# A hybrid decoder layer on one core: the mLSTM products in other PSUM banks, zeros and copies on GpSimd, attention's AV matmuls one step later

## The chip, the core and the metric

The kernel runs on one core of a Trainium2 chip. The core has TensorE (PE, matmuls into PSUM), VectorE (DVE), ScalarE (ACT), GpSimd (POOL) and SyncE (SP, which here only starts DMA transfers). Each engine works through its own list of instructions in order; semaphores let an instruction wait for another engine. PSUM has eight banks of 128 x 512 float32. The metric is the device time of one execution in microseconds, and the kernel before is the reference for it.

## What is computed

One decoder layer on 512 positions of width 1024, in float32. The normalised input goes through one projection; one group of its columns feeds four mLSTM heads, the other a sparse attention of eight heads whose keys an indexer selects (the 128 best of each query's past). Both results are concatenated, projected and added; a gated MLP with a short causal convolution and a last norm follow.

```python
h = rms_norm(x, norm_mix)
m_q, m_k, m_v, m_o, m_i, m_f, a_q, a_k, a_v, i_q, i_k, i_w = split_cols(h @ w_in, IN_SIZES)
qk = silu(causal_dwconv(concat(m_q, m_k), mlstm_conv_w, mlstm_conv_b))
hm = mlstm_chunkwise(q, k, v, m_i + i_bias, m_f + f_bias)       # 4 heads, 64 wide keys, 128 wide values
#   sc  = (q k^T / 8) * exp(dmat - m_t);  num = inter + sc v;  h = num / max(|den|, exp(-m_t))
hm = sigmoid(m_o) * rms_norm(hm, mlstm_norm)
ha = dsa_attention(a_q, a_k, a_v, i_q, rms_norm(i_k), i_w / sqrt(8), rel_bias)
#   score = sum_h relu(q_idx k_idx / 8) w;  top-k keys;  softmax(q k / 8 + bias) v
x = x + concat(hm, ha) @ w_out
u = causal_dwconv(rms_norm(x, norm_ffn) @ w_up, ffn_conv_w, ffn_conv_b)
out = rms_norm(x + (silu(gate) * val) @ w_down, norm_final)
```

## The kernel before

Matmuls run on pairs of rounded numbers: each float32 operand is split into a rounded high part and the rest (`split`, L121: ScalarE copies, VectorE or GpSimd subtracts), and three products make one. Weights come in pieces of 1 MB, are split into `whi` and `wlo`, and are used once. The 512 positions are four blocks (t = 0 to 3).

The order of the work is written out by hand. `merge` (L29) lays the steps of a main list (projection matmuls) and of side lists side by side: each side list has a range (a, b) as shares of the main list, and its steps are spread over it by their cost. What comes out is the order in which instructions are issued; each engine keeps it. So an instruction that waits holds up everything behind it on its engine. `later` holds small pieces (weight splits, convolution taps) that are issued after a step each.

PSUM banks come from rotating tags (L61): "mm" has two banks for projections, "lg" three, "tp" two, "av" one. A tile of a tag waits for the last reader of the tile that had the bank before.

Three stages matter here.

The stage of L734 to L744 ends with the first step of the attention loop (`ready`) and the first six of the 33 top-3 instructions (`top_steps(3)`: sixteen pairs of `max` and `match_replace` on VectorE over block 3's scores, then `keep`, the mask of the selected keys).

The stage of L857 to L862 has as its main list the mLSTM convolution projections and half of the values (24 steps); beside it run the other 27 top-3 instructions, the gates, two `decay` steps, and the attention loop `att_[1:]`. The loop has 32 items, one for each block t and head h. Its step i issues: the query halves for coming items (`queries`: ScalarE, GpSimd; `second`: the rounding rests, on VectorE into `qlz`, two at a time); the logits of item i on TensorE into a bank of "lg"; the transposes of item i-3 into "tp" and their copy to SBUF (pT, on ScalarE, for odd heads of block 3 on VectorE); the reduce of item i-1 on VectorE (L695) and its exponential on ScalarE (L698); for block 3 the score of item i on GpSimd (L704, bias plus mask, which the reduce of that item reads); and the AV matmuls of item i-4, followed after the eighth head by the division (L718).

The stage of L912 to L917 has 24 projection steps of twelve 256-column matmuls (the other half of the values, then the output gate). Beside it run two `decay` steps, `parts`, `qks` and four `to_mix`. `parts` first makes, for each of four heads, `keys(h)` (ScalarE copies, VectorE subtracts, giving kh) and then `queries(h)` (two ScalarE copies into the halves of qh, a VectorE subtract into ql); `zeros(h)` (L811) clears the other half of ql, heads 0 and 1 ahead of `keys(0)`, heads 2 and 3 behind `keys(3)`. `qks` has 16 products `qk(h, sb)`: two matmuls into one bank, and one or two multiplies on VectorE which read the bank. `to_mix` transposes an attention block into "tp" and splits it from there. The products and `to_mix` share "tp":

```python
pq = bank("tp")     # L844, in qk
pt = bank("tp")     # L906, in to_mix
```

Of the kernel before, what the change touches and what calls it, by code (L numbers as in the profile page):

```python
# [13 lines left out]
AF = mybir.ActivationFunctionType  # L14
# [30 lines left out]
def hybrid_layer(ctx: ExitStack, tc: tile.TileContext, a, out):  # L45
# [591 lines left out]
    def att_steps(ts):  # L637
# [21 lines left out]
        def step(i):  # L659
            if i % 4 == 1 and i // 4 + 1 < n // 4:  # L660
                queries(i // 4 + 1)
            if i and i % 2 == 0 and i // 2 + 1 < n // 2:
                second(i // 2 + 1)
            if i < n:
                t, h = items[i]
                w = (t + 1) * 128
# [21 lines left out]
            if 0 <= i - 1 < n:  # L688
                t, h = items[i - 1]
                w = (t + 1) * 128  # L690
                if h == 0:
                    rsum[t] = small.tile([128, 8], F32, name="rs")
                l = ap.tile([128, 512], F32, name="l", tag="wB", bufs=3)
                nm = small.tile([128, 1], F32, name="nm", bufs=4)
                nc.vector.tensor_tensor_reduce(l[:, :w], lg.pop(i - 1)[:, :w],  # L695
                                               backwards(bias["T"][:, h, :w]) if t < 3 else score[t], -1.0, 3.0e38,
                                               OP.add, OP.min, nm)
                nc.scalar.activation(l[:, :w], l[:, :w], AF.Exp, bias=nm, scale=-1.0,  # L698
                                     accum_out=rsum[t][:, h:h + 1])
                ll[i - 1] = l  # L700
            if i < n and items[i][0] >= 3:

                t, h = items[i]
                nc.gpsimd.tensor_tensor(score[t], backwards(bias["T"][:, h, :(t + 1) * 128]), keep[t], OP.add)  # L704
            if 0 <= i - 4 < n:
                t, h = items[i - 4]
                if h == 0:
                    pout[t] = bank("av")
                pT, po = lp.pop(i - 4), pout[t]
                for j in range(t + 1):  # L710
                    nc.tensor.matmul(po[:, h * 64:(h + 1) * 64], pT[:, j * 128:(j + 1) * 128],  # L711
                                     av[:, j, h * 64:(h + 1) * 64], start=(j == 0), stop=(j == t))
# [14 lines left out]
        def ready():  # L727
# [1 line left out]
            queries(0)  # L729
            second(0)  # L730
            second(1)
        return [ready] + [costed(i) for i in range(n + 4)]

    main = []  # L734
    for c in range(4):
# [46 lines left out]
    def weight_steps():  # L782
# [28 lines left out]
        def zeros(h):  # L811

            b_ = own[h % 2][1]
            if h == 2:
                ql["two"] = ap.tile([128, 2, S], F32R, name="mql", tag="mk")
            ql[h] = ql["two"][:, h - 2, :] if h >= 2 else ap.tile([128, S], F32R, name="mql", tag=("ql", "score3")[h])
            nc.scalar.activation(ql[h][b_].rearrange("p (t c) -> p t c", t=NB),
                                 ident[b_, None, :].to_broadcast([64, NB, 128]), AF.Copy, scale=0.0)

        def keys(h):  # L820
            if h == 0:
# [10 lines left out]
        def queries(h):  # L832
            a_, b_ = own[h % 2]
            qh[h], src = part(4 + h), mq[a_, h // 2, :]
            nc.scalar.activation(qh[h][a_], src, AF.Copy)
            nc.scalar.activation(qh[h][b_], src, AF.Copy)
            nc.vector.tensor_tensor(ql[h][a_], src, qh[h][a_].bitcast(F32), OP.subtract)

        def qk(h, sb):
# [1 line left out]
            n = (NB - sb) * 128  # L841
            t0 = min(sb * 128, 256)
            o, ks = sb * 128 - t0, slice(sb * 128, (sb + 1) * 128)
            pq = bank("tp")  # L844
            nc.tensor.matmul(pq[:, :S - t0], kh[h][:, ks], qh[h][:, t0:], start=True, stop=False)
            nc.tensor.matmul(pq[:, :S - t0], kh[h][:, ks], ql[h][:, t0:], start=False, stop=True)
            s_ = sc[:, sb * 128:(sb + 1) * 128]
# [11 lines left out]
    for c in range(4):  # L859
        main += fm_steps(H, to_conv(c))  # L860
    main += tm_steps(H, to_mv(0))
    merged(main, (0.0, 0.5, top3[6:]), (0.403, 0.74, gates_b), (0.781, 0.957, decays[:2]), (0.7, 0.7, [silus]), (0.007, 1.0, att_[1:]))  # L862


    def head_steps(pair):
# [47 lines left out]
    main = tm_steps(H, to_mv(1))  # L913
    for c2 in range(2):
        main += tm_steps(H, to_mo(c2))
    merged(main, (0.0, 0.05, decays[2:]), (0.08, 0.5, parts), (0.42, 1.0, qks),
           (0.16, 0.6, [lambda t=t: to_mix(ha[t], mixa, t) for t in range(NB)]))  # L917

    def gate_out(t):
# [202 lines left out]
```

## Time and profile before

| | value |
|---|---|
| time, three runs | 680.48 us median, 679.57 lowest, 1314.57 highest |
| profiled execution, its own time | 681.01 us |
| its span, from first to last instruction | 679.3 us |
| TensorE busy, share of the span | 656.2 us, 97% |
| VectorE busy | 398.9 us, 59% |
| ScalarE busy | 299.8 us, 44% |
| GpSimd busy | 147.5 us, 22% |
| mean granted clock of TensorE | 0.993 |
| slices of the span (of 40) with a granted clock under 0.9 | one, the fourteenth (about 221 to 238 us) |

Times of rows count from the span's start. "Busy" is the time in which an engine has an instruction in work; matmuls overlap, so a busy TensorE isn't at its peak. The granted clock is 1.00 at 2.4 GHz and 0.50 at 1.2 GHz. A row of a timeline has start and duration in us, engine, line, operation, written tile <- read tiles, shape, and how many instructions it stands for; in brackets, the idle time ahead of it and what ended that.

### The profile page before, as it was taken

The numbers are of one execution on the slowest core, as the hardware profiler recorded it, in microseconds if no ns is written. First come the engines' busy times: TensorE is split into PE (matmuls) and PEld (weight loads), VectorE is DVE, ScalarE is ACT, GpSimd is POOL, SyncE is SP. The second block draws the span as 40 slices with busy tenths as digits, with TensorE's granted clock in tenths as the row PEclk, the third lists the DMA queues.
The fourth block names the chain that finished last, engine by engine and source line by source line (L and its number), as shares of the span: only waits on it lengthen the run. The fifth ranks groups of instructions, "written<-read, shape, count | busy, mean of one in ns | idle before, by whom it ended". The sixth has DMA issues, their size and how long they took to land.

```text
span 679.3 us, 8957 instructions
## 1 busy us (share of the span) xinstructions
PE 656.2 (97%) x3455; PEld 560.0 (82%) x3455; DVE 398.9 (59%) x741; ACT 299.8 (44%) x516; POOL 147.5 (22%) x156
## 2 busy tenths in 40 slices
PE   7999999989999799999999999999999999999996
PEld 4987889778899698889888888888888888888885
DVE  4688999996656656656465655555555552222233
ACT  5555355655847424435434444445344441111223
POOL 2132576333430005314011010110101020000023
PEclk9999999999999799999999999999999999999999
DMA  9321533010111111132133213331233143323102
GB/s 305 115 65 62 190 122 124 0 64 11 52 63 63 62 64 62 35 122 68 58 123 119 67 63 125 124 106 54 89 124 123 66 152 124 124 73 114 62 32 93
DMA packets 47194, 62.22 MB, mean 92 GB/s; under 512 B 3795, under 2 KB 40855, under 8 KB 47152
## 3 DMA queue, kind: packets, MB, share of 16 engines
q1 hardware_dynamic: 45488, 56.83, 25.0%
q0 software_dynamic: 944, 3.25, 1.5%
q10 hardware_dynamic: 720, 1.57, 0.6%
q8 instruction: 27, 0.44, 0.3%
q14 instruction: 15, 0.12, 0.1%
HBM read 59.53 MB, written 2.12 MB: 91 GB/s over the span
## 4 chain that ended last, share of the span: by engine, by line
PE 74%; DVE 16%; ACT 4%; issue 3%; POOL 1%; DMA 1%; POOLq 0%; DVEq 0%; ACTq 0%
PE bank_mm L192 9%; PE bank_mm L193 9%; PE bank_mm L194 9%; PE bank_av L192 4%; PE bank_av L193 4%; PE bank_av L194 4%; DVE score L513 3%; DVE m L510 3%; DVE score L495 2%; PE bank_lg L1052 2%; PE bank_lg L1050 2%; PE bank_lg L1051 2%; PE bank_mm L363 2%; PE bank_av L711 2%; PE bank_mm L945 1%
## 5 line engine op out<-in xcount | busy, mean ns | idle before, releaser
L123 DVE TENSOR_TENSOR wlo<-raw,whi 128x1024 fp32r<-128x1024 f32 x78 | 96.7, 1244 | 121.5 <-ACT whi L122 121.5
L122 ACT ACTIVATE whi<-raw 128x1024 fp32r<-128x1024 f32 x100 | 104.9, 1051 | 95.2 <-PE bank_mm L1051 73.4
L192 PE MATMUL bank_mm<-fh,whi 128*128 128x512 f32 (+1 forms) x248 | 93.2, 376 | 0.0
L194 PE MATMUL bank_mm<-fh,wlo 128*128 128x512 f32 (+1 forms) x248 | 93.1, 376 | 0.0
L193 PE MATMUL bank_mm<-fl,whi 128*128 128x512 f32 (+1 forms) x248 | 93.1, 375 | 0.0
L1015 POOL TENSOR_TENSOR yc<-yc 128x512 f32<-128x512 f32 x22 | 28.4, 1291 | 213.4 <-DVE yc L999 213.4
L123 POOL TENSOR_TENSOR wlo<-raw,whi 128x1024 fp32r<-128x1024 f32 x22 | 54.2, 2465 | 75.9 <-ACT whi L122 58.6
L194 PEld LDWEIGHTS bank_mm<-fh,wlo 128*128 128x128 f32 x248 | 46.7, 188 | 8.5
L192 PEld LDWEIGHTS bank_mm<-fh,whi 128*128 128x128 f32 x248 | 46.7, 188 | 8.5
L193 PEld LDWEIGHTS bank_mm<-fl,whi 128*128 128x128 f32 x248 | 46.7, 188 | 8.3
L192 PE MATMUL bank_av<-fh,whi 128*128 128x512 f32 (+1 forms) x128 | 48.2, 376 | 0.0
L194 PE MATMUL bank_av<-fh,wlo 128*128 128x512 f32 (+1 forms) x128 | 48.1, 376 | 0.0
L193 PE MATMUL bank_av<-fl,whi 128*128 128x512 f32 (+1 forms) x128 | 48.1, 376 | 0.0
L122 ACT ACTIVATE gh<-yc 128x512 fp32r<-128x512 f32 x22 | 13.9, 632 | 69.2 <-POOL yc L1015 69.2
L192 PE MATMUL bank_mm<-hh,whi 128*128 128x512 f32 (+1 forms) x112 | 43.7, 390 | 0.0
L123 DVE TENSOR_TENSOR gl<-yc,gh 128x512 fp32r<-128x512 f32 x22 | 15.2, 693 | 47.4 <-ACT gh L122 47.4
L194 PE MATMUL bank_mm<-hh,wlo 128*128 128x512 f32 (+1 forms) x112 | 42.0, 375 | 0.0
L193 PE MATMUL bank_mm<-hl,whi 128*128 128x512 f32 (+1 forms) x112 | 42.0, 375 | 0.0
L236 PE MATMUL bank_mm<-whi,hh 128*128 128x256 f32 x112 | 33.0, 295 | 0.0
L1008 ACT ACTIVATE yc<-yc 128x512 f32<-128x512 f32 x22 | 13.9, 632 | 42.3 <-DVE yc L999 42.3
L237 PE MATMUL bank_mm<-whi,hl 128*128 128x256 f32 x112 | 32.0, 286 | 0.0
L238 PE MATMUL bank_mm<-wlo,hh 128*128 128x256 f32 x112 | 32.0, 286 | 0.0
(325 smaller groups left out, 1542.0 us busy)
## 6 DMA issues: line engine op xcount, KB each, us to landing
raw<-in_w_up_dram SPq DMA_DIRECT2D x22, 1024.0 KB, 5.1
raw<-in_w_in_dram SPq DMA_DIRECT2D x13, 1024.0 KB, 4.9
raw<-in_w_down_dram SPq DMA_DIRECT2D x11, 1024.0 KB, 4.9
raw<-in_w_out_dram SPq DMA_DIRECT2D x4, 1024.0 KB
T<-skew POOLq DMA_DIRECT2D x1, 2048.0 KB, 8.6
x<-in_x_dram SPq DMA_DIRECT2D x3, 512.0 KB, 5.3
out_dram<-xn SPq DMA_DIRECT2D x4, 256.0 KB, 2.1
out_dram<-xn ACTq DMA_DIRECT2D x4, 256.0 KB, 2.5
```

The costliest lines, as they stand in the source:

```text
L122: nc.scalar.activation(hv, src, AF.Copy)
L123: (eng or nc.vector).tensor_tensor(lv, src, hv.bitcast(F32), OP.subtract)
L192: nc.tensor.matmul(ps_, lh, rh, start=first, stop=False)
L193: nc.tensor.matmul(ps_, lh, rl, start=False, stop=False)
L194: nc.tensor.matmul(ps_, ll, rh, start=False, stop=last)
L236: nc.tensor.matmul(st["ps"], ah, wh[:, i, :], start=(k == 0), stop=False)
L237: nc.tensor.matmul(st["ps"], al, wh[:, i, :], start=False, stop=False)
L238: nc.tensor.matmul(st["ps"], ah, wl[:, i, :], start=False, stop=(k == 7))
L510: nc.vector.max(m8[0], acc)
L513: nc.vector.match_replace(acc, m8[0], acc, TAKEN)
L1008: nc.scalar.activation(ys[c][:, 0, :], ys[c][:, 0, :], AF.Silu)
L1015: nc.gpsimd.tensor_tensor(y[:, 0, :], y[:, 0, :], y[:, 1, :], OP.mult)
```

## The change

Five edits. In the attention loop `second` is issued after the reduce of the step, and the AV matmuls work on item i-5 in place of i-4, so that the loop has one step more. `zeros(h)` runs on GpSimd, and for heads 2 and 3 so does the second of the two query copies. The products take their bank from "lg". And three ranges move: top-3 to 0.57 from 0.5, `parts` to (0.05, 0.45) from (0.08, 0.5), `qks` to begin at 0.48 from 0.42.

```diff
--- before.py
+++ after.py
@@ -659,8 +659,6 @@
         def step(i):
             if i % 4 == 1 and i // 4 + 1 < n // 4:
                 queries(i // 4 + 1)
-            if i and i % 2 == 0 and i // 2 + 1 < n // 2:
-                second(i // 2 + 1)
             if i < n:
                 t, h = items[i]
                 w = (t + 1) * 128
@@ -698,15 +696,17 @@
                 nc.scalar.activation(l[:, :w], l[:, :w], AF.Exp, bias=nm, scale=-1.0,
                                      accum_out=rsum[t][:, h:h + 1])
                 ll[i - 1] = l
+            if i and i % 2 == 0 and i // 2 + 1 < n // 2:
+                second(i // 2 + 1)
             if i < n and items[i][0] >= 3:
 
                 t, h = items[i]
                 nc.gpsimd.tensor_tensor(score[t], backwards(bias["T"][:, h, :(t + 1) * 128]), keep[t], OP.add)
-            if 0 <= i - 4 < n:
-                t, h = items[i - 4]
+            if 0 <= i - 5 < n:
+                t, h = items[i - 5]
                 if h == 0:
                     pout[t] = bank("av")
-                pT, po = lp.pop(i - 4), pout[t]
+                pT, po = lp.pop(i - 5), pout[t]
                 for j in range(t + 1):
                     nc.tensor.matmul(po[:, h * 64:(h + 1) * 64], pT[:, j * 128:(j + 1) * 128],
                                      av[:, j, h * 64:(h + 1) * 64], start=(j == 0), stop=(j == t))
@@ -729,7 +729,7 @@
             queries(0)
             second(0)
             second(1)
-        return [ready] + [costed(i) for i in range(n + 4)]
+        return [ready] + [costed(i) for i in range(n + 5)]
 
     main = []
     for c in range(4):
@@ -814,8 +814,8 @@
             if h == 2:
                 ql["two"] = ap.tile([128, 2, S], F32R, name="mql", tag="mk")
             ql[h] = ql["two"][:, h - 2, :] if h >= 2 else ap.tile([128, S], F32R, name="mql", tag=("ql", "score3")[h])
-            nc.scalar.activation(ql[h][b_].rearrange("p (t c) -> p t c", t=NB),
-                                 ident[b_, None, :].to_broadcast([64, NB, 128]), AF.Copy, scale=0.0)
+            nc.gpsimd.tensor_scalar(ql[h][b_].rearrange("p (t c) -> p t c", t=NB),
+                                    ident[b_, None, :].to_broadcast([64, NB, 128]), 0.0, None, op0=OP.mult)
 
         def keys(h):
             if h == 0:
@@ -833,7 +833,10 @@
             a_, b_ = own[h % 2]
             qh[h], src = part(4 + h), mq[a_, h // 2, :]
             nc.scalar.activation(qh[h][a_], src, AF.Copy)
-            nc.scalar.activation(qh[h][b_], src, AF.Copy)
+            if h < 2:
+                nc.scalar.activation(qh[h][b_], src, AF.Copy)
+            else:
+                nc.gpsimd.tensor_copy(qh[h][b_], src)
             nc.vector.tensor_tensor(ql[h][a_], src, qh[h][a_].bitcast(F32), OP.subtract)
 
         def qk(h, sb):
@@ -841,7 +844,7 @@
             n = (NB - sb) * 128
             t0 = min(sb * 128, 256)
             o, ks = sb * 128 - t0, slice(sb * 128, (sb + 1) * 128)
-            pq = bank("tp")
+            pq = bank("lg")
             nc.tensor.matmul(pq[:, :S - t0], kh[h][:, ks], qh[h][:, t0:], start=True, stop=False)
             nc.tensor.matmul(pq[:, :S - t0], kh[h][:, ks], ql[h][:, t0:], start=False, stop=True)
             s_ = sc[:, sb * 128:(sb + 1) * 128]
@@ -859,7 +862,7 @@
     for c in range(4):
         main += fm_steps(H, to_conv(c))
     main += tm_steps(H, to_mv(0))
-    merged(main, (0.0, 0.5, top3[6:]), (0.403, 0.74, gates_b), (0.781, 0.957, decays[:2]), (0.7, 0.7, [silus]), (0.007, 1.0, att_[1:]))
+    merged(main, (0.0, 0.57, top3[6:]), (0.403, 0.74, gates_b), (0.781, 0.957, decays[:2]), (0.7, 0.7, [silus]), (0.007, 1.0, att_[1:]))
 
 
     def head_steps(pair):
@@ -913,7 +916,7 @@
     main = tm_steps(H, to_mv(1))
     for c2 in range(2):
         main += tm_steps(H, to_mo(c2))
-    merged(main, (0.0, 0.05, decays[2:]), (0.08, 0.5, parts), (0.42, 1.0, qks),
+    merged(main, (0.0, 0.05, decays[2:]), (0.05, 0.45, parts), (0.48, 1.0, qks),
            (0.16, 0.6, [lambda t=t: to_mix(ha[t], mixa, t) for t in range(NB)]))
 
     def gate_out(t):
```

Line numbers of the new kernel are 2 lower from L664 to L700, the same from there to L835, and 3 higher from L837. The order of instructions follows at three places.

The first place is TensorE in the third stage, where the products begin (`part` and `mql` are the parts of keys and queries; `bank_mm` and `bank_av` are projection banks). Before:

```order
L236 MATMUL bank_av<-whi,hh 128x256
L237 MATMUL bank_av<-whi,hl 128x256
L238 MATMUL bank_av<-wlo,hh 128x256
L845 MATMUL bank_tp<-part 128x512
L846 MATMUL bank_tp<-mql,part 128x512
L845 MATMUL bank_tp<-part 128x384
L846 MATMUL bank_tp<-mql,part 128x384
L236 MATMUL bank_av<-whi,hh 128x256
L237 MATMUL bank_av<-whi,hl 128x256
```

After, the first product:

```order
L238 MATMUL bank_av<-wlo,hh 128x256
L848 MATMUL bank_lg<-part 128x512
L849 MATMUL bank_lg<-mql,part 128x512
L236 MATMUL bank_mm<-whi,hh 128x256
L237 MATMUL bank_mm<-whi,hl 128x256
L238 MATMUL bank_mm<-wlo,hh 128x256
```

And after the twelve projection matmuls that begin there, the second and the third:

```order
L238 MATMUL bank_mm<-wlo,hh 128x256
L848 MATMUL bank_lg<-part 128x384
L849 MATMUL bank_lg<-mql,part 128x384
L911 MATMUL bank_tp<-ident,qv 128x128 x4
L848 MATMUL bank_lg<-part 128x256
L849 MATMUL bank_lg<-mql,part 128x256
L236 MATMUL bank_mm<-whi,hh 128x256
```

The first two products stood together on banks of "tp"; now a projection step stands between them, both are on "lg", and the fourth `to_mix` (L911, the only user of "tp") comes between the second and the third.

On ScalarE the same stage, from the third key copy to the third `to_mix` copy, before:

```order
L826 ACTIVATE part<-mk 64x512
L817 ACTIVATE mql<-ident 64x512 x2
L761 ACTIVATE mv<-bank_mm 128x2x128
L835 ACTIVATE part<-mq 64x512
L836 ACTIVATE part<-mq 64x512
L122 ACTIVATE mixa<-bank_tp 128x4x128
L835 ACTIVATE part<-mq 64x512
L836 ACTIVATE part<-mq 64x512
L122 ACTIVATE whi<-raw 128x1024 x2
L835 ACTIVATE part<-mq 64x512
L836 ACTIVATE part<-mq 64x512
L122 ACTIVATE mixa<-bank_tp 128x4x128
```

After:

```order
L826 ACTIVATE part<-mk 64x512
L761 ACTIVATE mv<-bank_av 128x2x128
L835 ACTIVATE part<-mq 64x512
L837 ACTIVATE part<-mq 64x512
L761 ACTIVATE mv<-bank_mm 128x2x128
L122 ACTIVATE mixa<-bank_tp 128x4x128
L835 ACTIVATE part<-mq 64x512
L837 ACTIVATE part<-mq 64x512
L835 ACTIVATE part<-mq 64x512
L122 ACTIVATE whi<-raw 128x1024 x2
L835 ACTIVATE part<-mq 64x512
L122 ACTIVATE mixa<-bank_tp 128x4x128 x2
```

The zeros (L817) are gone from between the key copies and the query copies, two of the second query copies (L836, now L837) as well, and the head-3 query copy (the last L835) stands ahead of the third `mixa` copy.

The second place is TensorE in the attention loop, one step of block 1 (the numbers tell tiles apart). Before, where pT_1513 is the copy of bank_tp_1510, transposed in the step before:

```order
L670 MATMUL bank_lg_1524<-kS_657,qd_1399 128x256
L671 MATMUL bank_lg_1524<-kS_657,ql_658 128x256
L673 LDWEIGHTS identb_356
L673 MATMUL bank_lg_1524<-keep1_366,identb_356 128x256
L681 MATMUL bank_tp_1528<-ident_117,l_1486 128x128 x2
L711 MATMUL bank_av_1490<-qv_84,pT_1513 128x64 x2
```

After, where pT_1524 is the copy of bank_tp_1521, and the step between has bank_tp_1547:

```order
L668 MATMUL bank_lg_1561<-kS_657,qd_1489 128x384
L669 MATMUL bank_lg_1561<-kS_657,ql_658 128x384
L671 LDWEIGHTS identb_356
L671 MATMUL bank_lg_1561<-keep2_367,identb_356 128x384
L679 MATMUL bank_tp_1565<-ident_117,l_1526 128x128 x2
L711 MATMUL bank_av_1507<-qv_84,pT_1524 128x64 x2
```

The AV matmul now reads what was transposed two steps before.

The third place is VectorE where `keep` of block 3 (keep_368) is written; L695, now L693, with T is a reduce of blocks 0 to 2, with score_365 of block 3. Before:

```order
L513 MATCH_REPLACE score_365<-m_1682,score_365 128x512
L516 TENSOR_SCALAR keep_368<-score_365 128x512
L755 SCALAR_TENSOR_TENSOR mk<-bank_mm,cw,mk 128x509
L695 ISA l,nm<-bank_lg,T 128x384
L695 ISA nm 128x1
L755 SCALAR_TENSOR_TENSOR mk<-bank_mm,cw,mk 128x510
L755 SCALAR_TENSOR_TENSOR mk<-bank_mm,cw,mk 128x511
L657 TENSOR_TENSOR ql<-qv,qd 64x128 x2
L695 ISA l,nm<-bank_lg,T 128x384
```

After:

```order
L510 MAX m_1750<-score_365 128x8
L513 MATCH_REPLACE score_365<-m_1750,score_365 128x512
L693 ISA l,nm<-bank_lg,T 128x384
L693 ISA nm 128x1
L516 TENSOR_SCALAR keep_368<-score_365 128x512
L693 ISA l,nm<-bank_lg,T 128x384
L693 ISA nm 128x1
L657 TENSOR_TENSOR ql<-qv,qd 64x128 x2
L693 ISA l,nm<-bank_lg,score_365 128x512
```

Before, four reduces of block 2 stood between `keep` and the first reduce that reads the score (two of them further down than is shown); now there is one.

## Rows read from the trace of the kernel before

**Rows 1.** Busy time by stretch: engine us (instructions), granted clock, DMA share, GB/s.
```profile
core 0: us, PE busy (x) PEld busy (x) DVE busy (x) ACT busy (x) POOL busy (x), PEclk, DMA share, GB/s
...
118.70:160.00 41.30, 37.61 (x230) 30.96 (x229) 37.74 (x115) 25.12 (x75) 11.75 (x15) 1.00 0.08 26
...
222.86:227.70 4.84, 0.00 (x1) 0.00 (x1) 3.94 (x6) 4.74 (x7) 0.00 (x0) 0.88 0.09 6
227.70:233.41 5.71, 5.71 (x25) 5.71 (x26) 2.83 (x8) 0.07 (x1) 0.00 (x0) 0.50 0.46 179
...
254.07:660.00 405.93, 405.93 (x1924) 340.86 (x1923) 202.56 (x276) 156.02 (x230) 58.17 (x67) 1.00 0.27 91
```

**Rows 2.** TensorE's waits, 118 to 250: who for whom, us, times, longest.
```profile
PE bank_tp L845 <- DVE mixa L123: 4.8, 1, 4.8
PE bank_av L711 <- ACT pT L686: 2.7, 4, 0.7
PE bank_lg L670 <- DVE nm L695: 1.0, 2, 0.6
PE bank_tp L681 <- ACT l L698: 0.8, 1, 0.8
PE bank_av L711 <- DVE qv L718: 0.4, 1, 0.4
```

**Rows 3.** Timeline of TensorE around the long wait.
```profile
227.70 0.69 PE L845 MATMUL bank_tp<-part 128*128 128x384 f32 x1 [4.84 <-DVE mixa L123]
...
228.51 0.41 PE L236 MATMUL bank_av<-whi,hh 128*128 128x256 f32 x1
...
231.07 0.41 PE L845 MATMUL bank_tp<-part 128*128 128x256 f32 x1
...
234.44 0.28 PE L236 MATMUL bank_mm<-whi,hh 128*128 128x256 f32 x1
...
235.87 0.41 PE L845 MATMUL bank_tp<-part 128*128 128x512 f32 x1
```

**Rows 4.** Timeline of ScalarE, 217.9 to 227.6.
```profile
217.99 1.27 ACT L817 ACTIVATE mql<-ident 64x512 fp32r<-64x512 f32 x2 [0.85 <-DVE part L827]
...
220.08 0.63 ACT L836 ACTIVATE part<-mq 64x512 fp32r<-64x512 f32 x1
...
225.87 0.60 ACT L122 ACTIVATE mixa<-bank_tp 128x512 fp32r<-128x512 f32 x1
```

**Rows 5.** Timeline of VectorE, 223.7 to 228.
```profile
224.90 0.42 DVE L767 COPY past<-bank_mm 128x256 f32<-128x256 f32 x1
...
226.97 0.67 DVE L123 TENSOR_TENSOR mixa<-bank_tp,mixa 128x512 fp32r<-128x512 f32 x1
```

**Rows 6.** Timelines of GpSimd and VectorE, 105 to 111, and GpSimd at 210.
```profile
105.70 1.51 POOL L634 TENSOR_SCALAR ql<-ident 128x512 fp32r<-128x512 f32 x1
...
106.23 0.69 DVE L621 TENSOR_TENSOR kS<-k__1054,kS 64x512 fp32r<-64x512 f32 x1
...
108.84 2.41 POOL L123 TENSOR_TENSOR wlo<-raw,whi 128x1024 fp32r<-128x1024 f32 x1 [0.71 <-PE bank_av L238]
108.93 2.46 DVE L657 TENSOR_TENSOR ql<-qv,qd 64x128 fp32r<-64x128 f32 x1
...
210.24 0.64 POOL L800 TENSOR_SCALAR_AFFINE_SELECT qv<-qv 128x512 f32<-128x512 f32 x1 [1.45 <-ACT qv L799]
```

**Rows 7.** Timeline of TensorE, 135 to 137, one attention step.
```profile
135.28 0.37 PE L670 MATMUL bank_lg<-kS,qd 128*128 128x256 f32 x1
...
135.72 0.38 PE L681 MATMUL bank_tp<-ident,l 128*128 128x128 f32 x2
136.84 0.41 PE L711 MATMUL bank_av<-qv,pT 128*128 128x64 f32 x2 [0.74 <-ACT pT L686]
```

**Rows 8.** Timelines of VectorE and GpSimd, 159 to 173: keep, score, its reduce.
```profile
159.11 0.43 DVE L516 TENSOR_SCALAR keep<-score 128x512 bf16<-128x512 f32 x1
...
167.86 1.18 POOL L704 TENSOR_TENSOR score<-T,keep 128x512 f32<-128x512 f32 x1
...
172.98 0.69 DVE L695 CUSTOM_DVE_ANT_0 l<-bank_lg,score 128x512 f32<-128x512 f32 x1
```

## The prediction

> **What bounds the kernel now.** I read the page first, then busy time by stretch, then TensorE's waits, then the timeline of the place that stands out. The stretches [rows 1] show where something can be won: from 254.07 to 660 us TensorE is busy for all 405.93 us, so what is won before 254 us is kept to the end, and nothing that this diff touches runs later. Up to 118.7 us both kernels issue the same rows. Between the two there are 41.30 us with TensorE busy for 37.61, a second half of the attention loop that is nearly full, then 4.84 us in which it does nothing, then 5.71 us at clock 0.50, the lower of its two levels (1.2 GHz).
>
> TensorE's waits of this part are five groups [rows 2]. One wait alone is 4.84 us: a product of `qk` (L845) for the subtract of `to_mix` (L123) on VectorE. The others, 2.7 + 1.0 + 0.8 + 0.4 = 4.9 us, belong to the attention loop: AV matmuls for the pT copy on ScalarE (four times), logits for a bank that VectorE has not reduced, one transpose for the exponential, one AV for the division.
>
> **What the 4.84 us are.** `qk` and `to_mix` both take "tp", which has two banks. The second product needs the bank of the third `to_mix`; that comes free when VectorE ends the subtract that starts at 226.97 and takes 0.67 [rows 5], and TensorE goes on at 227.70 [rows 3]. VectorE is late because ScalarE is: it copies that bank only at 225.87, after zeros, query copies, an earlier split and two weight splits in one unbroken queue from 217.99 [rows 4]. After the stall the clock is low: twelve 256-column matmuls take 231.07 - 228.51 = 2.56 us, the same twelve later 235.87 - 234.44 = 1.43 us [rows 3]. The low stretch lasts 5.71 us [rows 1], so it costs 5.71 x (1 - 1.43 / 2.56) = 2.5 us. The place costs 4.84 + 2.5 = 7.3 us in all.
>
> **Products in "lg", later.** "lg" has three banks, and in this stage only the four `decay` steps use it before. So the first three products find free banks whatever `to_mix` does, and the fourth needs the first one's. In the new order one more projection step (twelve matmuls, 1.43 us) stands ahead of the first product, which so ends at 222.86 + 1.43 = 224.3 in the old run's time. The fourth comes two steps of 1.43 us, two products and a group of transposes (some 0.8 us) later, near 227.9. Is the first bank read by then? In the old run VectorE read it straight after the subtract of 226.97. ScalarE's half of that split moves up: four zeros leave the queue ahead of it (two pairs of 1.27 us, whose starts overlap: 2.4 us) with the idle 0.85 us before the second pair, and one query copy of 0.63 us leaves while another moves in [rows 4]. So 225.87 becomes about 222.6. VectorE has one subtract (0.69 us for that shape, [rows 6]) and one bank copy (0.42, [rows 5]) more ahead of the read, and its weight splits in between; I put the read at 225 to 226.5, at least 1.4 us ahead of the fourth product. No wait takes the place of the stall, and without it I see no cause for the low clock, so I take the whole 7.3 us. The next thing to be late would be VectorE's copy of a projection bank: it came at 224.90 [rows 5], is needed again near 228, and moves up with the rest.
>
> **Zeros and copies on GpSimd.** A zeroing from the same source took 1.51 us there (L634, [rows 6]), against 0.63 on ScalarE [rows 4]. Four are 6.0 us. The two query copies I bound by ScalarE's 0.63 us from below and by 1.5 us from above, and take the upper end. GpSimd ends its last `affine_select` at 210.24 + 0.64 = 210.9 [rows 6]; zeros 0 and 1 then run to about 214, zeros 2 and 3 wait for the last key subtract and run to about 220, the copies to 223 at worst. The first product's second matmul needs the first block at about 224, head 2 comes many products later. That is ten microseconds of cover, and GpSimd has nothing else to do here. Cost: nothing; without the cover 1.5 us for each block.
>
> The trace has a warning for work that runs beside VectorE. While GpSimd did a two-input subtract (2.41 us from 108.84), a VectorE subtract with both inputs in SBUF took 2.46 us for a quarter of the elements of one that took 0.69. But that one of 0.69 us ran wholly inside GpSimd's zeroing of L634 [rows 6], which is work of the kind that is moved: one input. I go by this row. The Trainium skill ("SBUF — State Buffer", Who interferes with whom) makes no such difference: a VectorE instruction with two SBUF inputs contends with any GpSimd instruction that reads SBUF, and whoever issues second waits. By that rule the subtracts of this stage would be held up by the zeros, which is the third rival; the 2.46 us agree with it, the 0.69 us do not.
>
> **AV a step further back, `second` after the reduce.** The four pT waits are 0.7 us each. They stand where two attention steps follow one another without projection work: logits at 135.28, AV wanted at 136.10, begun at 136.84 [rows 7]. One step more is such a stretch of 0.8 us more, so all 2.7 us should go; if ScalarE is late by more than a step, none. `second` now runs behind the reduce of its step, so a reduce no longer waits for it, nor for a GpSimd instruction that blocks it. Of the logits' 1.0 us I keep half, because `max` and `match_replace` still stand among the reduces. At the exponential's wait (0.8) ScalarE ran a weight split and a bank copy first; in the new order the exponential comes ahead of them, and it goes. The division's 0.4 stays. Against this stands VectorE's load, 37.74 us in 41.30 [rows 1]: TensorE can't run much ahead of it. The range 0.57 for 0.5 spreads the same 27 top-3 instructions over 14% more work, which gives VectorE about what TensorE gains, and I take off 1.0 us. Sum 2.7 + 0.5 + 0.8 - 1.0 = 3.0 us, with bounds 0 and 4.9.
>
> The spread makes `keep` of block 3 late. It was written at 159.11; the score build (1.18 us on GpSimd) and the first reduce that needs it (172.98) came so much later that 12 us lay free between them [rows 8]. In the new order three more reduces, three convolution taps and a `second` stand ahead of `keep`, some 5 us of work, and one reduce lies between it and the one that needs it; the loop itself arrives some 4 us sooner, from the waits gone and from projection steps that now stand behind it. About 3 us of cover are left. I cost it at nothing, a miss at 1 to 2 us.
>
> **Sum.** The profiled execution took 681.0 us (span 679.3). 681.0 - 7.3 - 3.0 = 670.7. The median of the runs shown is 680.5, 0.5 lower: **670.2 us**.
>
> **Rivals.** First, the attention loop gives nothing: VectorE sets its pace and the waits form again. For it speaks VectorE at 91%; against it, that only 1.0 of the 4.9 us are waits on a reduce. 680.5 - 7.3 = 673.2.
>
> Second, the loop gives all 4.9: 680.5 - 7.3 - 4.9 = 668.3. For it, that nothing delays a reduce by a blocked subtract any more; against it, the division, which nothing touches.
>
> Third, the zeros block VectorE's subtracts. VectorE then loses 3.0 us to the first pair and up to 6.0 to the second with the copies. The cover of the fourth product is 1.4 us or more; VectorE waits for ScalarE in part of that time anyway. I price it at half, 4.5 us of new waiting on "lg", between 0 and 7.6: 670.2 + 4.5 = 674.7, and 677 if the clock falls again. Against it: the row of 0.69 us. The skill's rule above is this rival.
>
> Fourth, slower than before: `keep` comes so late that score build, reduce and block 3's first transposes form a chain with TensorE idle. Past the 3 us of cover each microsecond stalls TensorE for one, and a stall like that of 4.84 us brings 2.5 us of low clock. To end above 680.5 it has to lose 10.3 us, so `keep` would have to be near 11 us later than I expect. VectorE's list from 118.7 us up to it is some 45 us long, so it would have to slow by a quarter; only its busy share speaks for that.
>
> **Chances and range.** Forecast 0.70, with its own range 668.8 to 672.5; first rival 0.12, second 0.07, third 0.08, slower 0.03. The range reaches from 667.5 (the second rival, less 0.8 us for the runs' spread below their median) to 675.0 (the third) and leaves out less than 2 in 10. Two per cent, about what a measurement of this kernel can tell from no change, are 13.6 us; all waits and the low clock together are 12.2. So faster by over 2% has 0.04, slower 0.02, within 2% 0.94.
>
> **What would show it.** Right: no product waits for "tp" or "lg", the clock stays at 1.00 from 222 to 246 us, zeros of about 1.5 us on GpSimd with key and query subtracts still at 0.69, no AV wait for pT. Wrong: products that wait for the multiplies of `qk` on VectorE; key subtracts of over 1 us; logits or transposes of block 3 that wait behind GpSimd's score build; waits in the attention loop that still add up to over 3 us.

## The result

The changed kernel took 674.2 us (median of four executions, 673.4 to 674.9). The ratio to the kernel before is 0.9905, with a 95% interval of 0.9887 to 0.9924: faster, within two per cent, and inside the range. The kernel before had a median of 680.8 us beside it, with one of its four executions at 1314.57 us, and 680.5 without that one, so the gain is 6.3 to 6.6 us. The forecast was 10.3 us faster, and the missing 4 us are all in the attention loop. The profiled execution took 673.75 us, its span 672.0.

TensorE's waits of the kernel after, from 100 us on (who waits for whom, us in total, times, longest), answer to [rows 2]:

```profile
PE bank_av L711 <- DVE qv L718: 2.7, 2, 2.3
PE bank_lg L668 <- DVE nm L693: 1.6, 3, 0.6
```

Three of the five groups of before are gone: the 4.8 us of the products, the four waits for pT, the one for the exponential. The division's one wait of 0.4 is still there (0.40 us at 159.11, ahead of block 2; before, 0.41 at 156.14), and one of 2.25 us ahead of block 1 has come to it. The logits' 1.0 has become 1.6. Busy time by stretch of the kernel after (columns as in [rows 1]):

```profile
138.00:140.00 2.00, 1.66 (x8) 1.45 (x9) 2.00 (x7) 0.60 (x2) 0.00 (x0) 0.89 1.00 338
140.00:142.00 2.00, 2.00 (x9) 1.69 (x8) 1.40 (x5) 0.00 (x0) 0.00 (x0) 0.50 0.52 175
142.00:144.00 2.00, 2.00 (x10) 1.82 (x10) 0.43 (x2) 0.87 (x3) 0.00 (x0) 0.76 0.03 8
222.00:228.00 6.00, 6.00 (x50) 5.87 (x49) 5.96 (x11) 2.42 (x4) 2.86 (x2) 1.00 0.41 128
228.00:246.00 18.00, 18.00 (x145) 17.74 (x145) 10.74 (x31) 3.14 (x3) 0.00 (x0) 1.00 0.21 75
```

The mLSTM stage (last two lines) is full and at clock 1.00, where before there were 4.84 us of nothing and 5.71 us at 0.50. In its place the clock now falls to 0.50 in the loop, behind the long wait for the division. If a stretch at a fraction c of full speed loses its length times 1 - c, this costs 2 x 0.11 + 2 x 0.50 + 2 x 0.24 = 1.7 us. That is an estimate from above: the twelve matmuls of [rows 3] lost 44% at half speed, and TensorE did nothing for a part of the first of the three stretches.

In sums, the loop had 4.9 us of waits before. After, it has 2.7 + 1.6 = 4.3 us of waits and up to 1.7 us of low clock, 6.0 together, up to 1.1 more. The trace itself shows how much more. The same `decay` product (L785) stands at the beginning of the next stage, in the kernel before and after:

```profile
206.00 0.50 PE L785 MATMUL bank_lg<-cds,pick 64*128 64x512 f32 x1
```
```profile
206.40 0.50 PE L785 MATMUL bank_lg<-cds,pick 64*128 64x512 f32 x1
```

The same logits matmul at the loop's start begins at 118.71 before and 118.50 after. So the loop of this execution got 0.6 us longer. The forecast had it 3.0 us shorter.

Where the 2.7 us are, VectorE and then GpSimd and TensorE of the kernel after (timelines: start, us, in brackets the idle time ahead and who ended it):

```profile
135.48 0.41 DVE L693 CUSTOM_DVE_ANT_0 l<-bank_lg,T 128x256 f32<-128x256 f32 x1
...
135.82 1.43 DVE L657 TENSOR_TENSOR ql<-qv,qd 64x128 fp32r<-64x128 f32 x2
137.25 0.20 DVE L715 RECIPROCAL rr<-rs 128x8 f32<-128x8 f32 x1
137.59 0.69 DVE L718 TENSOR_TENSOR qv<-bank_av,rr 128x512 f32<-128x512 f32 x1
```
```profile
134.28 2.36 POOL L123 TENSOR_TENSOR wlo<-raw,whi 128x1024 fp32r<-128x1024 f32 x1 [7.58 <-PE bank_tp L679]
...
138.34 0.66 PE L711 MATMUL bank_av<-qv,pT 128*128 128x64 f32 x4 [2.25 <-DVE qv L718]
...
159.11 0.88 PE L711 MATMUL bank_av<-qv,pT 128*128 128x64 f32 x6 [0.40 <-DVE qv L718]
```

The division of block 0 (L715, L718) reads the one bank of "av", and the first AV matmul of block 1 writes it. Between reduce (L693) and division stands `second` (L657), two subtracts that take 1.43 us together, not 0.58; GpSimd's two-input weight subtract runs beside the first until 136.64.

### The profile page after: what moved, and what is told of

It reads as the page before. It is cut to its first block, busy times and chain, and to the rows that moved or that the text cites. A ratio compares the mean times of both kernels' runs of the same rounds, so it can differ in the third digit from the quotient of the medians.

```text
span 672.0 us, 8948 instructions
## 1 busy us (share of the span) xinstructions
PE 654.9 (97%) x3455; PEld 559.4 (83%) x3455; DVE 403.2 (60%) x741; ACT 296.3 (44%) x510; POOL 157.0 (23%) x162
## 4 chain that ended last, share of the span: by engine, by line
PE 78%; DVE 13%; issue 3%; POOL 2%; ACT 2%; DMA 1%; POOLq 0%; DVEq 0%; ACTq 0%
PE bank_mm L192 9%; PE bank_mm L194 9%; PE bank_mm L193 9%; PE bank_av L192 4%; PE bank_av L193 4%; PE bank_av L194 4%; DVE score L513 3%; DVE m L510 3%; DVE score L495 2%; PE bank_lg L1055 2%; PE bank_lg L1053 2%; PE bank_lg L1054 2%; PE bank_mm L363 2%; PE bank_av L711 2%; PE bank_mm L236 2%
```

## Experiments: the mLSTM stage

**The mLSTM part alone.** The kernel before with this part of the change (bank, zeros and copies on GpSimd, ranges); the attention loop untouched.

```diff
-            pq = bank("tp")
+            pq = bank("lg")
...
-            nc.scalar.activation(qh[h][b_], src, AF.Copy)
+            if h < 2:
+                nc.scalar.activation(qh[h][b_], src, AF.Copy)
+            else:
+                nc.gpsimd.tensor_copy(qh[h][b_], src)
...
-(0.08, 0.5, parts), (0.42, 1.0, qks)
+(0.05, 0.45, parts), (0.48, 1.0, qks)
```

> The kernel before with the mLSTM part of the change alone: products in lg, zeros and two heads' copies by GpSimd, the ranges of parts and products. The attention loop is as before (AV four behind, `second` ahead of the logits, top-3 range 0.5). Theory: this part is worth the forecast 7.3 us, so the change's attention part is worth about nothing: 680.8 - 7.3 = 673.5 us, and the profile shows the five waits of the loop of before and none behind 206 us. Rival (the attention part did give 1 to 3 us and the mLSTM part less): 675 to 677 us.

Measured: 673.02 us (672.91 to 673.08), ratio 0.9889 [0.9877, 0.9902], 7.6 us less than the 680.61 beside it. TensorE's waits are those of the loop of before, and none behind it:

```profile
PE bank_av L711 <- ACT pT L686: 2.7, 4, 0.8
PE bank_lg L670 <- DVE nm L695: 1.0, 2, 0.6
PE bank_tp L681 <- ACT l L698: 0.8, 1, 0.8
PE bank_av L711 <- DVE qv L718: 0.4, 1, 0.4
```

The stage gave what the forecast said (7.3), and the attention part as changed costs 674.16 - 673.02 = 1.1 us by the medians, or 0.7 by the two profiled executions (673.75 and 673.05). The intervals of the two ratios overlap, but all executions of this run (672.91 to 673.08) are shorter than all of the change (673.40 to 674.87). So a small loss is likely, and a gain of 3.0 us is ruled out.

**The bank alone.** Of the three edits only the first.

> The kernel before with one edit: the products of `qk` take their bank from lg. Zeros and copies stay on ScalarE, the ranges of parts and products as before. Theory (the shared banks alone made the 4.84 us and the low clock behind them): no product waits for `to_mix`, and what is left is a wait for the multiplies on VectorE, which here still stand behind the late split at 227 us: 0 to 1.5 us, or 673.0 to 675 us. Rival (ScalarE's queue is the cause, the bank only the place): the stall comes back at the fourth product or at a projection bank with 2.5 us or more and the clock falls: 677 us or more.

Measured: 674.94 us, ratio 0.9927 [0.9915, 0.994], 5.1 us less than before. One product waits, the fourth:

```profile
227.99 0.36 PE L845 MATMUL bank_lg<-part 128*128 128x256 f32 x1 [1.73 <-DVE sc L851]
```

Without the shared banks most of the stall is gone. What is left lies in the edits that this run doesn't have: with zeros and copies still in ScalarE's queue and the ranges as before, VectorE reads the first product 1.73 us late. The clock stays at 1.00 behind this wait.

**The rest without the bank.** Zeros and copies on GpSimd and the ranges; products in "tp".

> The run with the mLSTM part alone, but with the products left in tp: zeros and copies by GpSimd, and the ranges. Theory: the products share two banks with `to_mix`, and each to be written waits for a split or a multiply two banks back; the split of the third `to_mix` ends near 226 us, the product that needs its bank is due near 225: a wait of 1 to 2 us, possibly with a low clock behind it: 674 to 677 us. Rival (the shorter ScalarE queue alone is enough): 673.0 us, no wait on tp.

Measured: 674.18 us, ratio 0.9916 [0.9902, 0.9929]. In this stage one wait is listed, now of `to_mix` for a product's multiply:

```profile
PE bank_tp L911 <- DVE sc L854: 0.5, 1, 0.5
```

That wait is about half of the 1.2 us by which this run is slower than the mLSTM part alone; no other wait of this stage is listed. So either half removes most of the stall (5.1 and 5.8 us), and the two together 7.6. Bank and queue were two causes of one wait, not two gains to be added.

## Experiments: the attention loop

**`second` at its old place,** AV five behind.

```diff
+            if i and i % 2 == 0 and i // 2 + 1 < n // 2:
+                second(i // 2 + 1)
             if i < n:
                 t, h = items[i]
...
                 ll[i - 1] = l
-            if i and i % 2 == 0 and i // 2 + 1 < n // 2:
-                second(i // 2 + 1)
```

> The changed kernel with `second` put back ahead of the logits of its step; AV stays five items behind. Theory (`second` now stands ahead of block 0's division and delays it): the 2.25 us wait of the AV matmuls for the division at 138 us shrinks to 0.7 to 1.0 us, and the granted clock of 138 to 144 us is 1.00 again, which is worth 1.5 + 1.7 us; reduces wait for `second` again, so logits waits of 0.5 us more: 674.2 - 3.2 + 0.5 = 671.5 us. Rival (VectorE's load sets the loop's pace): the wait turns up elsewhere, 673.5 to 674.5 us, with PE waits of the loop still above 4 us.

Measured: 676.7 us, ratio 0.9944 [0.9931, 0.9957], slower than the change. I had the order wrong: at the head of step 12 `second` is still ahead of that step's division, and now it meets GpSimd's subtract (135.27 to 137.63) in full:

```profile
135.79 2.44 DVE L657 TENSOR_TENSOR ql<-qv,qd 64x128 fp32r<-64x128 f32 x2
...
138.94 0.69 DVE L718 TENSOR_TENSOR qv<-bank_av,rr 128x512 f32<-128x512 f32 x1
...
139.69 0.63 PE L711 MATMUL bank_av<-qv,pT 128*128 128x64 f32 x3 [3.29 <-DVE qv L718]
```

These 2.44 us, 1.86 more than the two subtracts take alone, are most of the wait of 3.29. A wait of 1.5 us of a later matmul (L585, at 173 us) for a pT copy is new as well, and the clock is at 0.50 from 140 to 142 us. That the place behind the reduce was better than this one speaks for the change's edit; that neither is good, the next run shows.

**`second` at the end of the step,** behind AV and division; the same two lines moved down.

> The changed kernel with `second` issued at the end of its step, behind AV and division; all else as changed. Theory: division ends near 136.8 in place of 138.28, AV of block 1 waits at most 0.8 us, no low clock behind it, and no reduce waits for `second`: 674.2 - 1.5 - 1.7 = 671.0 us. If only `second` and not the block by GpSimd was the cause it is the same. Rival (VectorE's load): 673.5 to 674.5 us. A loss is possible if the logits then wait for qlz: over 674.5 us, with a wait on ql in TensorE's list.

Measured: 671.31 us (670.5 to 672.4), ratio 0.9866 [0.9853, 0.9878]. The division starts straight after the reduce, and the wait falls from 2.25 to 0.81:

```profile
136.15 0.69 DVE L716 TENSOR_TENSOR qv<-bank_av,rr 128x512 f32<-128x512 f32 x1
136.76 0.96 DVE L657 TENSOR_TENSOR ql<-qv,qd 64x128 fp32r<-64x128 f32 x2
...
136.90 0.55 PE L709 MATMUL bank_av<-qv,pT 128*128 128x64 f32 x3 [0.81 <-DVE qv L716]
```

The low clock was there in the profiled execution (672.38 us; 0.50 from 138 to 140 us), so the expectation held in its sum and not in that part; two other executions took 670.5 and 670.6 us at a mean clock of 0.997. Nor did reduces gain: the logits wait 1.7 us for them, where it was 1.6 in the change. The 0.81 us matter for another reason. In the loop of before one of the pT waits stands at the same place [rows 7]. In the run with the mLSTM part alone the three rows are

```profile
135.63 0.69 DVE L718 TENSOR_TENSOR qv<-bank_av,rr 128x512 f32<-128x512 f32 x1
...
135.99 0.36 ACT L686 ACTIVATE pT<-bank_tp 128x256 f32<-128x256 f32 x1
...
136.47 0.63 PE L711 MATMUL bank_av<-qv,pT 128*128 128x64 f32 x4 [0.74 <-ACT pT L686]
```

The division ends at 136.32 and the pT copy at 136.35. The wait had two causes, 0.03 us apart, and the profile names the last. Taking pT away leaves the wait.

**AV four behind,** `second` behind the reduce as changed.

```diff
-if 0 <= i - 5 < n:
+if 0 <= i - 4 < n:
```

> The changed kernel with AV four items behind as before; `second` stays behind the reduce. With four, the division falls into a step of odd number, in which no `second` is issued. Theory: no wait of over 1 us for the division and clock 1.00 throughout, worth 3.2 us, but the pT waits of before come back (2.0 to 2.7 us): 673.0 to 673.7 us. Rival (the lag itself is worth what was forecast and the place of `second` nothing): 676 to 677 us.

Measured: 673.39 us (672.0 to 676.2). The division's wait is 0.74 us, as the theory said, since with four it falls into step 11, which has no `second`; pT waits of 1.0 us are back. But the agreement in time is not one in mechanism: a wait of 1.95 us for an exponential stands new at 187 us, and the clock falls at two places in the profiled execution (676.16 us, the longest of six). The run tells only that, with the rest as changed, the 2.25 us need the odd lag.

**A projection step between the blocks.** The loop's range moved by a hair, so that one projection step lies between steps 12 and 13 and between 20 and 21. First with `second` as changed, then with it at the end.

```diff
-(0.007, 1.0, att_[1:])
+(0.015, 1.0, att_[1:])
```

> The changed kernel as it is (`second` behind the reduce and so ahead of the division), with the loop's range begun at 0.015. Theory: the projection step of 1.4 us now between step 12 and 13 takes up most of the 2.25 us: 0.5 to 1.0 us of wait is left, the low clock goes or halves: 674.2 - 1.4 - 0.8 to 1.7 = 671 to 672 us. If `second` ahead of the division costs nothing once a projection step lies between: the same as the run before, 668.8 us. Rival (VectorE's pace): 673.5 to 674.5 us.

> The run with `second` at the step's end, and the attention loop's range begun at 0.015 in place of 0.007. With AV five behind, this puts a projection step of 1.4 us between the AV that ends a block (step 12, 20) and the AV that begins the next (13, 21), which shared a stretch without one. Theory (what is left at 134 to 142 us is the division between two steps without projection work): no wait for the division, clock 1.00 from 118 to 206 us, worth 0.8 + 1.7 us: 671.3 - 2.5 = 668.8 us. Rival (VectorE's pace): waits for reduces or transposes take its place, 670.5 to 672 us.

Measured: 671.04 us, ratio 0.9865 [0.9851, 0.9878], and 669.46 us (668.7 to 670.4), ratio 0.9847 [0.9834, 0.9861]. The first has 0.35 us of its division wait left, though `second` still takes 1.31 us beside GpSimd's subtract; its low clock has moved, to 0.71 from 188 to 190 us and 0.50 to 192. The second has no such wait, with these waits in all and a full TensorE around the place (columns of the stretches as above):

```profile
PE bank_lg L668 <- DVE nm L693: 1.3, 1, 1.3
PE bank_lg L785 <- DVE nm L693: 0.9, 1, 0.9
PE bank_tp L679 <- ACT l L696: 0.4, 1, 0.4
```
```profile
134.00:138.00 4.00, 4.00 (x29) 3.53 (x29) 3.82 (x15) 2.82 (x10) 2.62 (x3) 1.00 0.24 51
138.00:142.00 4.00, 4.00 (x31) 3.50 (x28) 3.53 (x11) 3.03 (x10) 0.00 (x0) 1.00 0.65 219
```

This version beats both kernels: 4.7 us under the change and 3.6 under the mLSTM part alone by the medians, 3.9 and 2.9 by the ratios, each of which goes by executions of the kernel before beside it. VectorE is busy for 3.82 of the 4 us there and TensorE doesn't wait, so VectorE's load by itself was not the bound.

**GpSimd's weight subtract with one input.** The changed kernel; the low part of one weight piece is left out.

```diff
+        if i == 20:
+            nc.scalar.activation(hv, src, AF.Copy)
+            nc.gpsimd.tensor_scalar(lv, src, 0.0, None, op0=OP.mult)
+        else:
             split(hv, lv, src, nc.gpsimd if i in on_pool else None)
```

> The changed kernel, where GpSimd's weight subtract at 134.28 us (two inputs from SBUF, 2.36 us) is a multiply of one input by zero: the low part of that one weight piece is left out, the matmuls that use it stay. Theory (the two-input work blocks `second`, which is part of the late division): the two subtracts of `second` at 135.8 us take 0.28 to 0.35 us each in place of 0.97 and 0.44, the division ends 0.8 us sooner, the AV wait falls from 2.25 to about 1.45 us; the low clock stays: 674.2 - 0.8 = 673.4 us. Rival (any GpSimd work that reads SBUF blocks them): `second` still takes 0.8 us or more beside it, wait and time as before, 674.2 us.

Measured: 671.2 us (671.1 to 674.2), ratio 0.988 [0.9863, 0.9898]. `second` takes 0.58 us and the wait falls by 0.84 us to 1.41, as expected:

```profile
135.68 0.58 DVE L661 TENSOR_TENSOR ql<-qv,qd 64x128 fp32r<-64x128 f32 x2
...
136.61 0.69 DVE L722 TENSOR_TENSOR qv<-bank_av,rr 128x512 f32<-128x512 f32 x1
...
137.36 1.12 PE L715 MATMUL bank_av<-qv,pT 128*128 128x64 f32 x4 [1.41 <-DVE qv L722]
```

But the rival was not put to the test: without the input from ScalarE the multiply ran at 126.66, long before `second`, which stood beside no GpSimd work at all. What is shown is the price of the block, 0.84 us of 2.25. The time fell by more; the mean clock was 0.997 in the three executions of 671.1 and 671.2 us and lower in the other two (last section).

**The mLSTM part and `second` at the end,** AV four behind, top-3 range 0.5.

> The run with the mLSTM part alone, and `second` at the step's end; AV four behind and the top-3 range 0.5 as before. Theory (with four the division falls into a step without `second`, so its place only frees reduces, and the pT waits of the lag of four stay): waits for reduces down by 0.5 to 1.0 us, 673.0 - 0.7 = 672.3 us, pT waits still 2 to 2.7 us. Rival (the gain of the run with `second` at the end was all in its place, the lag gives nothing): 670.5 to 671.3 us.

Measured: 674.44 us (672.1 to 675.0), ratio 0.9906 [0.9891, 0.9921]: a miss, no gain over 673.02. The profiled execution (672.07) is the shortest of the five; the others had a mean clock of 0.992 to 0.995 and left no trace. In it the waits add up to 4.1 us. Half of it is one wait, ScalarE and TensorE:

```profile
178.82 1.28 ACT L771 ACT_TABLE_LOAD   x1
180.12 1.06 ACT L771 ACTIVATE mq<-mq 128x1024 f32<-128x1024 f32 x1
...
183.36 1.28 ACT L696 ACT_TABLE_LOAD   x1
184.65 0.72 ACT L696 ACTIVATE l<-l,nm 128x512 f32<-128x512 f32 x1
...
185.52 0.66 PE L679 MATMUL bank_tp<-ident,l 128*128 128x128 f32 x4 [1.95 <-ACT l L696]
```

The exponential of item 27 stands behind two Silu passes (the second isn't shown) with a table load on either side. The same 1.95 us stood in the run with AV four behind. That the loop ran into them by being early is a reading that no run tests. In the runs with AV five behind no wait for an exponential was over 0.6 us.

**The range from 0.020,** `second` at the end, AV five behind.

> The best run so far (`second` at the end, AV five behind, loop from 0.015), with the loop's range from 0.020. The divisions still have a projection step behind them; the three steps 5, 6, 7 that stood together are split. Theory: the 1.3 us wait of the logits for a reduce at 131.7 us was due to VectorE having three steps' reduces at once, and shrinks to 0.6 us: 668.7 us. Rival (it is VectorE's pace, the wait only moves): 669.5 us, waits of the loop again 2.5 us in all.

Measured: 669.44 us (667.8 to 671.1), ratio 0.9834 [0.982, 0.9847]. The 1.3 us wait is gone, and 1.9 us of waits are left in the loop, but the time is that of 0.015. The profiled execution (671.12, the longest of five) had the clock low from 186 to 194 us, at 0.50 from 188 to 192. Whether it is better stays open: the intervals overlap.

**AV four behind with a projection step between the blocks.** `second` at the end, range from 0.030.

> `second` at the end, AV four behind, loop from 0.030, which puts a projection step between the AV that ends a block and the one that begins the next (11 and 12, 19 and 20, 27 and 28), as 0.015 does with AV five behind. Theory (what counts is whether projection work lies between the two, not how far behind AV runs): no wait for the division, clock 1.00 in the first half of the loop; pT waits of up to 1.0 us may stay: 669.5 to 670.5 us. Rival (the lag of five is worth the 2.7 us of pT waits): 672 us. Block 3's exponential may come late behind ScalarE's two Silu passes, as in the other run with AV four behind and the wider top-3 range; then 672 us or more with a wait near 187 us.

Measured: 671.56 us (671.5 to 671.6), ratio 0.9871 [0.9857, 0.9884]. No wait for the division, clock 1.00 through the whole loop, as the theory said. But its other half falls, that the lag doesn't matter:

```profile
PE bank_av L709 <- ACT pT L684: 3.2, 4, 1.2
PE bank_lg L669 <- DVE ql L657: 1.0, 1, 1.0
PE bank_lg L668 <- DVE nm L693: 0.2, 1, 0.2
```

Against the run with AV five behind and a projection step at the same place (2.6 us of waits, 669.46) the pT waits are back, and the time is 2.1 us longer, 1.6 by the ratios. So the lag of five is worth some 2 us where nothing else takes its place, somewhat less than the 2.7 of the forecast; the two runs differ in the beginning of the range too. The 1.0 us for ql is the price that `second` at the end can have.

## Why the forecast was right and wrong, point by point

**The mLSTM stage, 7.3 us: right.** Measured 7.6 by itself. The first product starts at 224.06, the fourth at 228.41, and the first bank is read from 226.42 to 227.16; the loop being 0.4 us late, that is 223.7, 228.0 and 226.0 to 226.8 on the scale of the forecast (about 223.7, 227.9, 225 to 226.5). The fourth product so had 1.2 us to spare where 1.4 or more was said. The low clock went with the stall, as taken.

**Zeros and copies on GpSimd, nothing: right,** with sizes at the upper end: three of four zeros take 1.49 us, one 1.99, the copies 1.49 each. The third rival, VectorE blocked by them, did not come true, though the query subtracts did not all stay at 0.69 (last section).

**`keep`, nothing: right, with less cover than said.** TensorE waits neither for it nor for the score. VectorE and GpSimd of the kernel after:

```profile
166.41 1.99 DVE L516 TENSOR_SCALAR keep<-score 128x512 bf16<-128x512 f32 x1
...
170.29 0.69 DVE L693 CUSTOM_DVE_ANT_0 l<-bank_lg,score 128x512 f32<-128x512 f32 x1
```
```profile
165.73 2.39 POOL L123 TENSOR_TENSOR wlo<-raw,whi 128x1024 fp32r<-128x1024 f32 x1 [10.47 <-ACT whi L122]
168.48 1.17 POOL L704 TENSOR_TENSOR score<-T,keep 128x512 f32<-128x512 f32 x1 [0.36 <-DVE keep L516]
```

`keep` takes 1.99 us beside GpSimd's two-input subtract where it took 0.43 [rows 8]. The score is written at 169.65, and the reduce that reads it begins at 170.29: 0.6 us of cover, where about 3 were forecast.

**The attention loop, 3.0 us: wrong, and outside its bounds of 0 and 4.9.** The failed step is the one that counts the pT waits as gone and says of the division that its 0.4 stays, which puts no division wait in pT's place. The 0.4 did stay; 2.25 us came to it, ahead of block 1, where one of the pT waits had stood [rows 7]. The forecast asked what the fifth step of lag does to pT, and not into which step it puts the division. `second` is issued in even steps. Four behind, the AV of a block's last head falls into step 11, 19 or 27; five behind, into 12, 20 or 28. The change puts the division behind a `second` that it never met before. Two more things made the wait long: the GpSimd block (0.84 us of the 2.25, by the run with one input), and that steps 12 and 13 have no projection work between them (1.9 us of the 2.25, by the run with the range from 0.015). These two overlap and can't be added.

The other terms of this step: the pT waits, 2.7 us, went as said, and the exponential's 0.8 too. But the pT wait of [rows 7] had the division 0.03 us behind it as a second cause. The half of the logits' 1.0 that was to go did not; it became 1.6. In the runs with AV four behind and the loop from 0.007 the logits wait 0.3 to 1.0 us, with AV five behind 1.6 to 1.8, wherever `second` stands, so this came with the lag; why stays open. The 1.0 us taken off for VectorE's load has no run of its own, for none moves the top-3 range alone. The low clock of up to 1.7 us was in no term of the loop. Summed: -2.7 - 0.8 + 2.3 + 0.6 + 1.7 = +1.1 at the most, where the trace shows 0.6 and the medians against the mLSTM part alone 1.1.

**The rivals.** The time lies between two of them, the third (674.7), 0.5 us away, and the first (673.2), 1.0 away. Neither came true as told. The third had the zeros block VectorE, with waits for "lg" in the mLSTM stage, which has none; GpSimd did block VectorE, but in the loop and with a two-input subtract that both kernels have. The first (the loop gives nothing) has its sign, "waits that still add up to over 3 us", with 4.3. Its reason is not there: it had VectorE's load as the bound, and the version with `second` at the end and the projection step between the blocks ran some 4 us faster than the change with the same work on VectorE.

The time misses the forecast's own range (668.8 to 672.5). It lies within the whole range because the mLSTM term was right and the range reached up to the third rival's price. That the loop's loss, which no term foresaw, still fits into it is luck.

## What to carry to other kernels

When an edit shifts a step of a software pipeline, list what else is issued in the step that it lands in, on each engine, and what is issued in the same step number modulo the period of the other work. A wait names only its last releaser: before it is booked as a gain, see who else would have ended it at nearly the same time. And give the one-bank hand-over between two blocks a stretch of independent matmuls; moving a range by less than a hundredth did that here, and gave about 3 us where the change's edits of the loop lost about 1.

## What the runs showed of the hardware

**The clock can fall behind short waits, and not in every execution.** After the change it fell behind a wait of 2.25 us; with `second` at the end it fell behind waits of 0.60 and 0.81 us in a row, while behind the 1.73 us of the run with the bank alone it stayed at 1.00. In the two runs with the range from 0.015 nearly the same two waits stand at 186 to 188 us: 0.81 and 0.35 us, with the clock at 0.50 behind them, and 0.95 and 0.35, with the clock at 1.00. The run with one input had executions of 671.07, 671.13 and 671.2 us at a mean clock of 0.997, and 673.35 and 674.24 at 0.995 and 0.993; in the last, the profiled one, it was low from 136 to 144 us. What decides was not settled. Times of one kernel spread by up to 4 us, and the longer ones mostly have the lower mean clock.

**One-input work on GpSimd didn't block VectorE's two-input subtracts, but it isn't free.** GpSimd and VectorE of the kernel after:

```profile
211.35 3.06 POOL L817 TENSOR_SCALAR mql<-ident 64x512 fp32r<-64x512 f32 x2
...
221.88 3.04 POOL L839 CAST part<-mq 64x512 fp32r<-64x512 f32 x2
```
```profile
211.54 3.07 DVE L123 TENSOR_TENSOR wlo<-raw,whi 128x1024 fp32r<-128x1024 f32 x2 [2.35 <-ACT whi L122]
...
220.72 0.77 DVE L840 TENSOR_TENSOR mql<-mq,part 64x512 fp32r<-64x512 f32 x1 [0.47 <-ACT part L835]
221.67 1.23 DVE L123 TENSOR_TENSOR wlo<-raw,whi 128x1024 fp32r<-128x1024 f32 x1 [0.18 <-ACT whi L122]
...
224.48 0.99 DVE L840 TENSOR_TENSOR mql<-mq,part 64x512 fp32r<-64x512 f32 x1
```

The weight splits of 211 us, in the kernel before, with nothing on GpSimd:

```profile
211.15 2.44 DVE L123 TENSOR_TENSOR wlo<-raw,whi 128x1024 fp32r<-128x1024 f32 x2 [2.35 <-ACT whi L122]
```

Beside the zeros the two splits take 3.07 us, beside nothing 2.44; one split beside a copy takes 1.23, as much as alone. One query subtract takes 0.77 beside a zeroing and one 0.99 beside a copy, and another beside zeros 0.69, as alone. That is up to 0.3 us for each, far from the 2.44 us that two subtracts of a quarter of the elements took beside a two-input one. The Trainium skill ("SBUF — State Buffer", Who interferes with whom) has any VectorE instruction with two SBUF inputs contend with a GpSimd instruction that reads SBUF, and the later of the two fully blocked. The 2.44 us agree with it; these rows show a stretch and no exclusive wait.
